# The chunk states of the S5 layers with the inputs held and the table streamed, in two column halves

## The chip, the cores and the metric

The kernel runs on one core of a Trainium2 chip. The metric is device time in microseconds (us) of one execution; the median of three executions of the kernel before is 1205.5 us. TensorE (PE) multiplies, VectorE (DVE) and ScalarE (ACT) do the elementwise work, GpSimd (POOL) a little of it, and the queue of SyncE (SP) starts most transfers.

## What is computed

A network of four layers on 256 tokens of 1024 channels, all in float32. Layers 0 and 3 mix tokens with an S5 state-space mixer, layer 1 with differential attention, layer 2 with pooling; an MLP with a hidden width of 4096 follows each. The S5 mixer, cut to what matters here:

```python
u = h @ w_in                                   # 256 x 1024, 64 groups of 16 channels
bu = einsum('btgh,gph->btgp', u, bbar)         # 64 complex states in each group
x = scan over the tokens of  x[t] = abar * x[t-1] + bu[t]
y = einsum('btgp,ghp->btgh', x.re, c_re) - einsum('btgp,ghp->btgh', x.im, c_im) + d_skip * u
z = gelu(y);  out = (z * sigmoid(z @ w_gate)) @ w_out
```

## The kernel before

The kernel cuts the 256 tokens into 64 chunks of four tokens. For a chunk, a table takes its four inputs to the state that they alone produce; a scan then carries the states over the 64 chunks; a second table takes the carried state, and a third the chunk's own inputs, to the four outputs. Two groups of channels make a pair (2 x 64 states); the 32 pairs are worked in four quarters q of eight pairs.

The order of the work in an S5 layer is written out by hand in the string `SEQ` (line 87); `step` (line 763) emits one word after the other. The words that are spoken of below, each for a quarter q: `g` is half of the product with W_in (`gemm_quarter`, line 239), `V` turns its output into rows of channels (ACT line 794, DVE line 795), `i`, `o`, `s` build tables, `S` turns the state table on TensorE (16 transposes, line 595) and copies it out on ACT (line 598), `T` makes the third table (matmuls at line 618, ACT at 623 and 626, DVE at 624), `m` computes the chunk states (`s5_state`, line 672), `c` carries them (`s5_chain`, line 683), all on DVE, `y` makes the outputs (`s5_out`, line 711: eight times one matmul with T and two with O, one for each half of the 128 output rows, then gelu on ACT at 725 and transposes on DVE at 729), and `z` transposes these on TensorE (copies on ACT at 753). For a half of the columns, `e` is a quarter of the product with W_gate and `w` of that with W_out. In layer 3 the tables are built during earlier MLPs; `K`, `H`, `L` bring them back from memory.

Matmuls go through the helper `mm` (line 142), transposes through `tr` (146), elementwise DVE work through `tt` (151), so most rows of the profile have one of these lines. TensorE executes in the order of `SEQ`; the orders of ACT, DVE and SP are set when the kernel is built, and each engine runs its own list strictly in turn. A matmul of two plain float32 operands appears in the trace as two records, called passes below. The products with large weights are done with operands split in two parts on ACT (line 204) and DVE.

In `s5_state` a slice of the state table is the stationary operand and the chunk inputs V move, 64 columns of them:

```python
self.mm(ps[:, 64 * j:64 * j + 64], self.st[q % 2][:, :, 2 * j + ri], V[:, :, j], start=True, stop=True)
```

The table lies as `st = [128, 128, 16]`, so that a slice `[:, :, 2j + ri]` takes every 16th element of a partition. The result has the states in its 128 rows, as `c` wants it.

Of the kernel before, what the change touches and what calls it, by code (L numbers as in the profile page):

```python
# [16 lines left out]
NT = 2  # L17
# [22 lines left out]
def plan():  # L40
    """Half blocks of 256 rows x 512 columns (array, index, row, column) in the order in which they are used."""
# [34 lines left out]
def whole(name, i, row):  # L76
    """Whether a half block is taken whole instead of split."""
    return name == "s5_w_in" and i == 0 or name == "s5_w_gate" and row < GW[i]


# The order of emission in the S5 layers (0, 1: layers 0 and 3) and in attention (2).
# S5, for the quarter q of the channels: f transposes of the input, p parameters, i/o/s tables and S/T their parts on
# the tensor engine, K/H/L tables brought back, g W_in, V its output in rows of channels, m states, c carries, y outputs,
# z transposes; for the half n of the columns: e gate, w W_out.
# Attention: g and w the products with W_qkv and W_o, l lambda, r transposes, a scores and softmax, t transposes,
# b products with the values, n transposes of the result.
SEQ = {2: "g0 g0 g2 g0 g0 l g2 g2 g2 r00 g1 r20 g1 r01 r21 a01 a00 a10 g1 a11 g3 g3 t00 g1 t01 t10 g3 g3 g4 g4 r10 r30 r31 r11 t11 a02 a13 a03 g4 g4 b00 b01 a12 t03 g5 g5 t13 b11 n00 b10 t02 g5 g5 b03 t12 b13 n10 b02 b12 w0 w1 n01 w1 n11 w0 w0 w0 w1 w1",
       0: "f0 g0 p g2 i0 f1 g1 g0 s0 g1 S0 i1 V0 V1 s1 m0 o1 o0 S1 T0 g2 c0 m1 i2 c1 y0 T1 g3 o2 V2 S2 g3 i3 V3 y1 s2 T2 z0 m2 o3 e0 c2 z1 e1 T3 S3 s3 m3 c3 y2 e1 e0 z2 y3 e0 z3 e1 e0 e1 w0 w0 w0 w1 w0 w1 w1 w1",
       1: "g0 g3 g0 T0 K0 K1 V0 g1 m0 T1 g1 K2 V1 g2 g2 m1 c0 V2 c1 y0 g3 H2 m2 V3 c2 y1 K3 z0 m3 L2 z1 H3 c3 L3 e0 e1 y2 e0 e1 z2 y3 e0 z3 e1 e0 e1 w1 w0 w0 w0 w0 w1 w1 w1"}


class Net:
# [69 lines left out]
    def exp(self, out, x, shape, tag):  # L162
        """exp on the vector engine: 2^n times a polynomial of the rest, its even and its odd terms apart."""
# [26 lines left out]
    def fetch(self):  # L190
        """Loads and splits the half blocks [128, 2, 512] that come next."""
# [23 lines left out]
    def mm3(self, out, sh, sl, mh, ml, start, stop):  # L215
        """out += (sh + sl)^T (mh + ml), of which sl^T ml is below float32's rounding."""
# [6 lines left out]
    def gemm_unit(self, xT, u, banks, first, last):  # L223
        """Both token tiles times a half block of 256 x 512."""
# [14 lines left out]
    def gemm_quarter(self, xT, bank, first, last):  # L239
        """Both token tiles times 512 x 256, side by side in one bank."""  # L240
# [14 lines left out]
    def gemm_T_unit(self, xT, u, banks, first, last):  # L255
        """banks[f // 2][:, f % 2] += (half block of 256 x 512)^T xT for its four column tiles f."""
# [35 lines left out]
    def stat(self, t, n):  # L292
        """The squares of x[t][:, n half] towards the mean square; after both, 1 / rms."""
# [15 lines left out]
    def normed(self, n, t, sub, delay=1.5):  # L309
        """x[t][:, n half] is final for sublayer sub: its operands and statistics."""  # L310
# [11 lines left out]
    def first(self, n):  # L322
        """The same for a half of the input, in whole operands."""
# [80 lines left out]
    def rounded(self, out, a, s):  # L404
        """The integer nearest to a * s."""
# [11 lines left out]
    def s5_put(self, l, q):  # L417
        """Keeps the tables in memory until their layer."""
# [8 lines left out]
    def s5_get(self, l, q, part):  # L427
        """Brings back the tables of one stage: states and inputs (0), carries (1), outputs (2)."""
# [16 lines left out]
    def s5_params(self, l, P):  # L445
        """The discretised parameters, [128 = two groups x 64 states, 32 pairs of groups]."""
# [46 lines left out]
        # powers 4 .. 0 of the discretised eigenvalues, and the factor of the inputs  # L493
# [51 lines left out]
    def products(self, b, wa, wb):  # L545
        """b[0] times wa and b[1] times wb: b [128, 8, 16] over columns and powers, wa and wb [128, 8, 2, 4] over channels."""
# [8 lines left out]
    def s5_in_table(self, l, P, q):  # L555
        """From the inputs of a chunk to its state, for the eight pairs of groups 8 q .. (S)."""
# [21 lines left out]
    def swapped(self, l, q):  # L578
        """Whether the table of the states goes through memory to be turned."""
        return l == 1  # L580

    def s5_late(self, l, q, d=None):
        """The parts of the tables that the tensor engine makes: S from the inputs to the state, T to the outputs."""
# [5 lines left out]
        def states():  # L589
            st = self.st[q % 2]  # L590
            for ri in range(2):
                for b in range(2):
                    ps = self.bank()
                    for j in range(4):
# [36 lines left out]
    def s5_out_table(self, l, P, q):  # L631
        """From the state before a chunk to its outputs."""
# [16 lines left out]
    def s5_small_tables(self, l, P, q):  # L649
        """Phases of the chunks, e^{4 i theta (c - 32)}, and the decay over a chunk, zero where a pair begins."""  # L650
# [21 lines left out]
    def s5_state(self, l, P, q, V):  # L672
        """Eight pairs: the states that the chunks reach, from zero."""
        tb = P[q]
        tb["sb"] = []
        for ri in range(2):
            ps = self.bank()
            for j in range(8):
                self.mm(ps[:, 64 * j:64 * j + 64], self.st[q % 2][:, :, 2 * j + ri], V[:, :, j], start=True, stop=True)
                self.pe(0.213)  # L680
            tb["sb"].append(ps.rearrange("p (j c) -> p j c", j=8))

    def s5_chain(self, l, P, q):
        """Eight pairs: the states carried over the chunks, before each chunk."""
# [26 lines left out]
    def s5_out(self, l, P, q, V):  # L711
        """Eight pairs: outputs, gelu, and the transposes into rows of tokens."""
# [20 lines left out]
    def s5_z(self, l, P, q, zT, zf):  # L733
        """Transposes into rows of channels, as an operand and whole."""
# [20 lines left out]
    def s5(self, l, done):  # L755
# [7 lines left out]
        def step(c, q):  # L763
# [493 lines left out]
```

## Time and profile before

| | |
|---|---|
| times of three executions | 1204.42, 1205.5, 1205.73 us |
| span of the profiled execution | 1204.5 us |
| its TensorE: busy, mean granted clock | 97% of the span, 0.953 |
| its DVE, ACT busy | 67%, 55% |
| chain that ended last: share of TensorE | 94% |
| layer 0's S5 part, layer 3's S5 part | about 22 to 181 us, 866 to 1006 us |

The time of the profiled execution itself is not among the three; its span lies within their range, and the median is 1.0 us above it. The page's first part gives busy time by engine. In the chain of waits each step is followed back to what released it. The timeline lists instructions in order of time with start and length in us, and "x16" merges 16 records. [...]

### The profile page before, as it was taken

How to read it: one execution, taken by the hardware profiler on the slowest of the kernel's cores; microseconds unless marked ns; L12 is line 12 of the kernel's file. 1: busy time of each engine (PE TensorE's matmuls, PEld its weight loads, DVE VectorE, ACT ScalarE, POOL GpSimd, SP SyncE). 2: the span in 40 equal slices, each digit the busy share in tenths (PEclk: the TensorE clock that was granted, in tenths of full speed). 3: DMA queues.
4: the chain of work that ended last, by engine and by line, in shares of the span. 5: the costliest groups of instructions: out<-in, count | busy, mean ns of one | idle time of the engine just before them, and what ended most of it. 6: DMA issues, size and time to landing. Idle time of an engine off the chain costs nothing.

```text
span 1204.5 us, 18922 instructions
## 1 busy us (share of the span) xinstructions
PE 1171.1 (97%) x7192; PEld 1042.7 (87%) x7192; DVE 809.9 (67%) x1488; ACT 663.4 (55%) x1322; POOL 52.3 (4%) x111
## 2 busy tenths in 40 slices
PE   5999999999999999999999999999999999999994
PEld 4989889899888788989888899899898889989983
DVE  7766579857658997986655765655764766655563
ACT  4846367656656676775644754544630156554452
POOL 4002000000000001000000100000100001000000
PEclk9877799999999999999999999999985799999998
DMA  5211256766665444667667365665542256556651
GB/s 150 88 35 36 84 179 188 228 219 208 207 208 168 140 143 154 198 207 217 192 189 232 98 201 180 186 185 185 174 132 79 89 172 195 183 182 189 183 185 58
DMA packets 56635, 196.51 MB, mean 163 GB/s; under 512 B 7136, under 2 KB 7648, under 8 KB 56544
## 3 DMA queue, kind: packets, MB, share of 16 engines
q1 hardware_dynamic: 54528, 189.69, 50.5%
q10 hardware_dynamic: 2016, 5.61, 1.4%
q8 instruction: 56, 0.92, 0.3%
q14 instruction: 35, 0.29, 0.1%
HBM read 188.46 MB, written 6.82 MB: 162 GB/s over the span
## 4 chain that ended last, share of the span: by engine, by line
PE 94%; ACT 2%; DMA 1%; DVE 1%; issue 0%; SPq 0%; POOL 0%; ACTq 0%; POOLq 0%
PE mlp_ps L142 60%; PE mix_ps L142 31%; PE mix_ps L146 2%; DMA start_raw<-in_wts 1%; ACT start_st L598 0%; PE mlp_ps L146 0%; ACT mix_m L885 0%; ACT start_T L626 0%; ACT start_T L623 0%; DVE mix_m L151 0%; SPq L1071 0%; ACT mlp_m L1170 0%; DVE start_x L151 0%; ACT start_ba L575 0%; ACT mix_m L794 0%
## 5 line engine op out<-in xcount | busy, mean ns | idle before, releaser
L151 DVE TENSOR_TENSOR mlp_wlo<-mlp_raw,mlp_whi 128x512 fp32r<-128x512 f32 x492 | 318.5, 686 | 215.9 <-ACT mlp_whi L204 215.7
L204 ACT CAST mlp_whi<-mlp_raw 128x512 fp32r<-128x512 f32 x492 | 281.5, 618 | 255.3 <-PE mlp_ps L142 190.9
L142 PE MATMUL mlp_ps<-mlp_whi,mlp_m 128*128 128x512 f32 x1024 | 327.8, 396 | 0.0
L142 PEld LDWEIGHTS mlp_ps<-mlp_whi,mlp_m 128*128 128x128 f32 x1024 | 192.8, 188 | 45.5
L142 PE MATMUL mlp_ps<-mlp_m,mlp_whi 128*128 128x256 f32 x1248 | 226.2, 283 | 0.0
L142 PE MATMUL mlp_ps<-mlp_wlo,mlp_m 128*128 128x512 f32 x512 | 202.9, 396 | 0.0
L142 PEld LDWEIGHTS mlp_ps<-mlp_m,mlp_whi 128*128 128x128 f32 x1248 | 192.1, 188 | 0.6
L142 PE MATMUL mlp_ps<-mlp_m,mlp_wlo 128*128 128x256 f32 x624 | 175.2, 281 | 0.0
L142 PE MATMUL mlp_ps<-mix_m,mlp_whi 128*128 128x256 f32 x672 | 122.1, 283 | 0.0
L142 PEld LDWEIGHTS mlp_ps<-mlp_m,mlp_wlo 128*128 128x128 f32 x624 | 118.3, 190 | 0.0
L142 PEld LDWEIGHTS mlp_ps<-mlp_wlo,mlp_m 128*128 128x128 f32 x512 | 96.5, 188 | 22.0
L142 PE MATMUL mix_ps<-mix_whi,mix_m 128*128 128x512 f32 (+1 forms) x352 | 108.7, 385 | 0.0
L151 DVE TENSOR_TENSOR mix_wlo<-mix_raw,mix_whi 128x512 fp32r<-128x512 f32 x124 | 81.5, 685 | 38.4 <-ACT mix_whi L204 38.3
L204 ACT CAST mix_whi<-mix_raw 128x512 fp32r<-128x512 f32 x124 | 72.6, 621 | 62.0 <-PE mix_ps L142 35.0
L142 PEld LDWEIGHTS mlp_ps<-mix_m,mlp_whi 128*128 128x128 f32 x672 | 104.5, 188 | 1.8
L142 PE MATMUL mlp_ps<-mix_m,mlp_wlo 128*128 128x256 f32 x336 | 94.5, 281 | 0.0
L142 PEld LDWEIGHTS mix_ps<-mix_whi,mix_m 128*128 128x128 f32 x352 | 66.3, 195 | 13.3 <-issue 0.5
L142 PE MATMUL mix_ps<-mix_wlo,mix_m 128*128 128x512 f32 (+1 forms) x176 | 67.1, 381 | 0.0
L151 DVE TENSOR_TENSOR mlp_m<-mlp_m,mlp_m 128x512 fp32r<-128x512 f32 (+1 forms) x72 | 51.5, 716 | 19.4 <-ACT mlp_m L360 18.6
L142 PEld LDWEIGHTS mlp_ps<-mix_m,mlp_wlo 128*128 128x128 f32 x336 | 63.8, 190 | 0.0
L142 PE MATMUL mix_ps<-mix_m,start_st 128*128 128x64 f32 x256 | 56.9, 398 | 0.4 <-ACT start_st L598 0.3
L142 PEld LDWEIGHTS mix_ps<-mix_m,start_st 128*128 128x128 f32 x256 | 56.4, 311 | 0.9 <-ACT start_st L598 0.9
(324 smaller groups left out, 1523.5 us busy)
## 6 DMA issues: line engine op xcount, KB each, us to landing
mlp_raw<-in_wts SPq DMA_DIRECT2D x252, 512.0 KB, 4.1
mix_raw<-in_wts SPq DMA_DIRECT2D x84, 512.0 KB, 3.6
kept<-mlp_m SPq DMA_DIRECT2D x4, 512.0 KB
start_st<-kept SPq DMA_DIRECT2D x32, 64.0 KB, 3.3
start_x<-in_x SPq DMA_DIRECT2D x4, 256.0 KB
start_raw<-in_wts SPq DMA_DIRECT2D x2, 512.0 KB, 16.8
mlp_m<-in_s5bc SPq DMA_DIRECT2D x2, 512.0 KB, 4.6
kept<-start_O ACTq DMA_DIRECT2D x2, 512.0 KB
```

The source lines that it names most:

```text
L142: i = self.nc.tensor.matmul(*a, **k)
L146: i = self.nc.tensor.transpose(*a)
L151: (eng or self.nc.vector).tensor_tensor(out=out, in0=a, in1=b, op=op)
L204: nc.scalar.copy(hi[:, s], raw[:, s])
```

## The change

The chunk inputs become the stationary operand, 64 columns for a pair, and 256 columns of the table (two parts of 128) move. Two pairs j are put into the lower and the upper 64 columns of the array, and so into rows 0 to 63 and 64 to 127 of one bank; a quarter has eight matmuls of 256 columns instead of sixteen of 64. The result has chunks in its rows; ACT copies it to memory, and a new step `n` (`s5_turn`) turns it with eight transposes. The table is laid out so that 32 neighbours of a moving row lie together, V so that a pair's 64 columns do. In both `SEQ` strings `n` stands some words behind its `m`, and some `c`, `e`, `m` and `y` change places.

```diff
-       0: "... s1 m0 o1 o0 S1 T0 g2 c0 m1 i2 c1 y0 T1 g3 o2 V2 S2 g3 i3 V3 y1 s2 T2 z0 m2 o3 e0 c2 z1 e1 T3 S3 s3 m3 c3 y2 e1 e0 z2 y3 e0 z3 ..."
-       1: "g0 g3 g0 T0 K0 K1 V0 g1 m0 T1 g1 K2 V1 g2 g2 m1 c0 V2 c1 y0 g3 H2 m2 V3 c2 y1 K3 z0 m3 L2 z1 H3 c3 L3 e0 e1 y2 e0 e1 z2 y3 ..."
+       0: "... s1 m0 o1 o0 S1 n0 T0 m1 c0 g2 n1 i2 c1 y0 T1 g3 o2 V2 S2 g3 i3 V3 y1 s2 T2 m2 z0 o3 e0 n2 c2 z1 e1 T3 S3 s3 m3 e1 n3 c3 y2 e0 z2 y3 e0 z3 ..."
+       1: "g0 g3 g0 T0 K0 K1 V0 g1 m0 T1 g1 n0 K2 V1 g2 m1 c0 g2 n1 V2 c1 y0 g3 H2 m2 V3 y1 n2 K3 c2 z0 m3 L2 z1 H3 e0 n3 c3 L3 e1 y2 e0 e1 z2 y3 ..."
...
-                    nc.scalar.copy(st.rearrange("p m (j x) -> p j m x", x=2)[:, 4 * b:4 * b + 4, :, ri],
-                                   ps.rearrange("p (j m) -> p j m", j=4))
+                    nc.scalar.copy(st.rearrange("p a (j x) c -> p j x a c", x=2)[:, 4 * b:4 * b + 4, ri],
+                                   ps.rearrange("p (j a c) -> p j a c", j=4, a=4))
...
     def s5_state(self, l, P, q, V):
+        P[q]["rows"] = S = self.m4([128, 4, 2, 128])
+        for b in range(2):
+            ps = self.bank()
+            for i in range(2):
+                for r in range(2):
+                    j = 4 * b + 2 * i + r
+                    self.mm(ps[64 * r:64 * r + 64, 256 * i:256 * i + 256], V[:, j],
+                            self.st[q % 2][:, :, 2 * j:2 * j + 2].rearrange("p a x c -> p x a c"),
+                            start=True, stop=True, skip_group_check=True)
+                self.pe(0.43)
+            self.nc.scalar.copy(S[:, 2 * b:2 * b + 2].rearrange("p i x m -> p (i x m)"), ps)
+
+    def s5_turn(self, l, P, q):
         tb = P[q]
         tb["sb"] = []
         for ri in range(2):
             ps = self.bank()
-            for j in range(8):
-                self.mm(ps[:, 64 * j:64 * j + 64], self.st[q % 2][:, :, 2 * j + ri], V[:, :, j], start=True, stop=True)
-                self.pe(0.213)
+            for i in range(4):
+                self.tr(ps[:, 128 * i:128 * i + 128], tb["rows"][:, i, ri], self.ident)
+                self.pe(0.113)
...
-                V[q] = self.m2([128, NT, 8, 32])
+                V[q] = self.m2([128, 8, 64])
...
-        self.st = [self.t([128, 128, 16], f"st{b}") for b in range(2)]
+        self.st = [self.t([128, 4, 16, 32], f"st{b}") for b in range(2)]
```

Line numbers of the changed kernel are one to seventeen higher. The built order shows what an engine's list became.

TensorE in layer 0, from the state table of quarter 0 to `y0` (`start_st` is the state table, the first operand is the one that moves; `mix_cad` belongs to `T`). Before:

```order
L142 MATMUL mix_ps_457<-mix_m_125_431,start_st_17_95 128x64 x8
L142 MATMUL mix_ps_466<-mix_m_125_431,start_st_17_95 128x64 x8
L146 MATMUL mix_ps_499<-start_ident_65,start_ba_16_94 128x128 x4
L146 MATMUL mix_ps_505<-start_ident_65,start_ba_16_94 128x128 x4
L146 MATMUL mix_ps_511<-start_ident_65,start_ba_16_94 128x128 x4
L146 MATMUL mix_ps_517<-start_ident_65,start_ba_16_94 128x128 x4
L142 MATMUL mix_ps_525<-mix_cad_487,start_ba_15_93 32x64 x16
```

and after the change:

```order
L143 MATMUL mix_ps_458<-start_st_17_95,mix_m_125_431 64x256 x4
L143 MATMUL mix_ps_464<-start_st_17_95,mix_m_125_431 64x256 x4
L147 MATMUL mix_ps_494<-start_ident_65,start_ba_16_94 128x128 x4
L147 MATMUL mix_ps_500<-start_ident_65,start_ba_16_94 128x128 x4
L147 MATMUL mix_ps_506<-start_ident_65,start_ba_16_94 128x128 x4
L147 MATMUL mix_ps_512<-start_ident_65,start_ba_16_94 128x128 x4
L147 MATMUL mix_ps_518<-start_ident_65,mix_m_134_457 128x128 x4
L147 MATMUL mix_ps_523<-start_ident_65,mix_m_134_457 128x128 x4
L143 MATMUL mix_ps_530<-mix_cad_482,start_ba_15_93 32x64 x16
```

Sixteen matmuls of 64 columns became eight of 256 on half the rows, and the eight transposes of `n0` stand behind those of `S1` and ahead of `T0`.

DVE in layer 0 between `V1` and `c0` (`mix_q_pa`, `mix_q_pb` and `mix_cad` mark the products of the tables `o1` and `o0`; the rows with `mix_ps` begin the carry `c0`; the row on `start_T` is an addition to table T):

```order
L810 STREAM_TRANSPOSE mix_m_127_437<-mix_m_128_438 128x8x32
L158 TENSOR_SCALAR mix_m_130_444<-mix_m_129_443 128x512
L152 TENSOR_TENSOR mix_m_129_443<-mix_m_129_443,mix_m_130_444 128x512
L152 TENSOR_TENSOR mix_m_138_473<-start_m_7_75,mix_q_pa_269 128x1024
L152 TENSOR_TENSOR mix_m_139_474<-start_m_7_75,mix_q_pb_270 128x1024
L152 TENSOR_TENSOR mix_m_141_485<-start_m_7_75,mix_q_pa_269 128x1024
L152 TENSOR_TENSOR mix_cad_470<-mix_m_138_473,mix_m_139_474 128x16x64
L152 TENSOR_TENSOR mix_m_142_486<-start_m_7_75,mix_q_pb_270 128x1024
L152 TENSOR_TENSOR mix_cad_482<-mix_m_141_485,mix_m_142_486 128x16x64
L152 TENSOR_TENSOR mix_m_154_566<-mix_ps_518,mix_ph_383 128x1024
L152 TENSOR_TENSOR start_T_21_99<-start_T_21_99,mix_dd_528 32x16x16
L152 TENSOR_TENSOR mix_m_155_567<-mix_ps_523,mix_ph_383 128x1024
```

All six products now stand between the phases of quarter 1 and `c0`; before the change four of them stood ahead of V's first transposes, and the addition to T behind c0's scans instead of between its first two rows.

ACT in layer 0 behind `T2` and the gelu of `y1` (line 685 copies the rows of `m2`, 768 those of `z0`, which `e0` reads; 576, 627 and 660 to 666 build tables of quarters 2 and 3):

```order
L685 COPY mix_m_203_831<-mix_ps_832 128x512
L576 COPY start_ba_16_94<-mix_m_189_749 64x64x16 x2
L627 COPY start_T_21_99<-start_T_21_99 32x16x48
L627 COPY start_T_21_99<-start_T_21_99 32x16x32
L660 ACTIVATE mix_m_198_794<-mix_m_196_792 128x512
L664 ACT_TABLE_LOAD
L664 ACTIVATE mix_ph_799<-mix_m_196_792 128x512
L665 ACTIVATE mix_ph_799<-mix_m_198_794,start_hpi_88 128x512
L666 ACTIVATE mix_ph_799<-mix_m_196_792 128x512
L627 COPY start_T_21_99<-start_T_21_99 32x16x16
L685 COPY mix_m_203_831<-mix_ps_838 128x512
L768 COPY mix_m_207_849<-mix_ps_844 128x512
```

Before the change the copy of `z0` stood first in this stretch, directly behind T2's second activation.

## Rows read from the trace of the kernel before

**Rows 1.** The page, part 1: busy time, share of the span and instructions of each engine.
```profile
PE 1171.1 (97%) x7192; PEld 1042.7 (87%) x7192; DVE 809.9 (67%) x1488; ACT 663.4 (55%) x1322; POOL 52.3 (4%) x111
```

**Rows 2.** The chain that ended last, in order of time: start, length, engine, count.
```profile
867.92 0.87 PE mix_ps L146 x8
868.80 64.65 PE mix_ps L142 x404
```

**Rows 3.** The state table's tile: duration in ns (min/median/max), first and last start.
```profile
L142 PEld LDWEIGHTS mix_ps<-mix_m,start_st x256: 291/311/338, 38.4 to 940.8; 128*128 128x128 f32 x128
...
L598 ACT COPY start_st<-mix_ps x16: 1005/1070/1130, 37.3 to 116.6; 128x512 f32<-128x512 f32 x16
```

**Rows 4.** Stretches: length, then PE, PEld, DVE, ACT, POOL busy; granted clock; DMA, GB/s.
```profile
866.00:878.50 12.50, 12.50 (x107) 12.41 (x106) 10.14 (x23) 8.87 (x23) 2.97 (x7) 1.00 0.53 169
878.50:885.50 7.00, 7.00 (x34) 6.93 (x32) 2.64 (x4) 1.14 (x2) 0.00 (x0) 0.86 0.27 77
885.50:889.00 3.50, 3.50 (x33) 3.38 (x32) 2.45 (x2) 0.00 (x0) 0.00 (x0) 0.50 0.31 96
905.20:913.40 8.20, 8.20 (x50) 6.36 (x49) 7.01 (x6) 0.00 (x0) 0.13 (x1) 0.50 0.21 64
950.30:955.30 5.00, 5.00 (x50) 3.90 (x48) 3.98 (x6) 0.00 (x0) 0.00 (x0) 0.99 0.37 111
```

**Rows 5.** Timeline of TensorE: a `g` in whole operands (16 passes); `T3` (32 passes).
```profile
51.70 3.72 PE L142 MATMUL mix_ps<-mix_raw,mix_m 128*128 128x256 f32 x16
110.93 1.97 PE L142 MATMUL mix_ps<-mix_cad,start_ba 128*32 128x64 f32 x32
```

**Rows 6.** Timeline of TensorE, 950.62 to 950.65 us: the passes that had begun.
```profile
950.63 0.28 PE L142 MATMUL mix_ps<-mix_m,start_O 128*64 128x64 f32 x2
```

**Rows 7.** Timeline of TensorE inside `y2`, at the full clock.
```profile
951.52 0.43 PE L142 MATMUL mix_ps<-mix_m,start_T 128*128 128x64 f32 x2
951.89 0.34 PE L142 MATMUL mix_ps<-mix_m,start_O 128*64 128x64 f32 x4
952.15 0.32 PE L142 MATMUL mix_ps<-mix_m,start_T 128*128 128x64 f32 x1
```

**Rows 8.** Timeline of ACT in layer 0: copies, activations, a table load.
```profile
41.05 3.76 ACT L645 COPY start_O<-mix_cad 64x512 f32<-64x512 f32 x6
51.81 1.25 ACT L623 ACTIVATE start_T<-mix_ps,start_gmask 32x512 f32<-32x512 f32 x2 [1.10 <-PE mix_ps L142]
53.59 1.87 ACT L626 COPY start_T<-start_T 32x768 f32<-32x768 f32 x3
96.08 2.10 ACT L575 COPY start_ba<-mix_m 64x1024 f32<-64x1024 f32 x2
100.74 1.28 ACT L663 ACT_TABLE_LOAD   x1
107.58 0.59 ACT L753 COPY mix_m<-mix_ps 128x512 f32<-128x512 f32 x1 [1.39 <-PE mix_ps L146]
```

**Rows 9.** Timeline of DVE: V1's transposes; first and last instructions of the carry `c3`.
```profile
37.12 0.81 DVE L795 STREAM_TRANSPOSE mix_m<-mix_m 128x256 f32<-128x256 f32 x2 [0.45 <-ACT mix_m L794]
943.36 2.35 DVE L151 TENSOR_TENSOR mix_m<-mix_ps,mix_ph 128x1024 f32<-128x1024 f32 x2
...
951.60 2.75 DVE L151 TENSOR_TENSOR mix_m<-mix_m,mix_m 64x504 f32<-64x504 f32 x4
```

**Rows 10.** Timeline of TensorE: the starts of `y0`, `e0`, `y3` in layer 0, `y0`, `y3` in layer 3.
```profile
62.07 0.64 PE L142 MATMUL mix_ps<-mix_m,start_T 128*128 128x64 f32 x2
101.61 5.49 PE L142 MATMUL mix_ps<-mix_m,mix_raw 128*128 128x256 f32 x16
140.60 0.33 PE L142 MATMUL mix_ps<-mix_m,start_T 128*128 128x64 f32 x2
905.23 0.64 PE L142 MATMUL mix_ps<-mix_m,start_T 128*128 128x64 f32 x2
964.39 0.33 PE L142 MATMUL mix_ps<-mix_m,start_T 128*128 128x64 f32 x2
```

More of the change, by code (lines that the diff above doesn't have):

```diff
@@ L87 @@
 SEQ = {2: "g0 g0 g2 g0 g0 l g2 g2 g2 r00 g1 r20 g1 r01 r21 a01 a00 a10 g1 a11 g3 g3 t00 g1 t01 t10 g3 g3 g4 g4 r10 r30 r31 r11 t11 a02 a13 a03 g4 g4 b00 b01 a12 t03 g5 g5 t13 b11 n00 b10 t02 g5 g5 b03 t12 b13 n10 b02 b12 w0 w1 n01 w1 n11 w0 w0 w0 w1 w1",
-       0: "f0 g0 p g2 i0 f1 g1 g0 s0 g1 S0 i1 V0 V1 s1 m0 o1 o0 S1 T0 g2 c0 m1 i2 c1 y0 T1 g3 o2 V2 S2 g3 i3 V3 y1 s2 T2 z0 m2 o3 e0 c2 z1 e1 T3 S3 s3 m3 c3 y2 e1 e0 z2 y3 e0 z3 e1 e0 e1 w0 w0 w0 w1 w0 w1 w1 w1",
-       1: "g0 g3 g0 T0 K0 K1 V0 g1 m0 T1 g1 K2 V1 g2 g2 m1 c0 V2 c1 y0 g3 H2 m2 V3 c2 y1 K3 z0 m3 L2 z1 H3 c3 L3 e0 e1 y2 e0 e1 z2 y3 e0 z3 e1 e0 e1 w1 w0 w0 w0 w0 w1 w1 w1"}
+       0: "f0 g0 p g2 i0 f1 g1 g0 s0 g1 S0 i1 V0 V1 s1 m0 o1 o0 S1 n0 T0 m1 c0 g2 n1 i2 c1 y0 T1 g3 o2 V2 S2 g3 i3 V3 y1 s2 T2 m2 z0 o3 e0 n2 c2 z1 e1 T3 S3 s3 m3 e1 n3 c3 y2 e0 z2 y3 e0 z3 e1 e0 e1 w0 w0 w0 w1 w0 w1 w1 w1",
+       1: "g0 g3 g0 T0 K0 K1 V0 g1 m0 T1 g1 n0 K2 V1 g2 m1 c0 g2 n1 V2 c1 y0 g3 H2 m2 V3 y1 n2 K3 c2 z0 m3 L2 z1 H3 e0 n3 c3 L3 e1 y2 e0 e1 z2 y3 e0 z3 e1 e0 e1 w1 w0 w0 w0 w0 w1 w1 w1"}
 class Net:
@@ L566, in s5_in_table @@
             self.halves(lambda g, p: nc.scalar.copy(ba[p].rearrange("p j x k g h -> p (j x) k g h")[:, :, 3, g], d[p, :, 3]))
-            m = self.m4([128, 2, 32, 16])
-            nc.vector.transpose(out=m.rearrange("p i c f -> p f i c"),
+            m = self.m4([128, 2, 16, 32])
+            nc.vector.transpose(out=m.rearrange("p i f c -> p f i c"),
                                 in_=d.rearrange("p f (i k) h -> p f i (k h)", i=2))
             self.count += 1
-            P["swap", q] = self.dram.tile([128, 2, 32, 16], F32, name=f"kept_{self.count}")
+            P["swap", q] = self.dram.tile([128, 2, 16, 32], F32, name=f"kept_{self.count}")
             nc.sync.dma_start(out=P["swap", q], in_=m)
@@ L597, in states @@
                         self.pe(0.113)
-                    nc.scalar.copy(st.rearrange("p m (j x) -> p j m x", x=2)[:, 4 * b:4 * b + 4, :, ri],
-                                   ps.rearrange("p (j m) -> p j m", j=4))
+                    nc.scalar.copy(st.rearrange("p a (j x) c -> p j x a c", x=2)[:, 4 * b:4 * b + 4, ri],
+                                   ps.rearrange("p (j a c) -> p j a c", j=4, a=4))
         def fetch():
             st = self.st[q % 2]
-            kept = self.tables[l]["swap", q].rearrange("(b k h) i c f -> b k h i (c f)", b=4, k=2)
+            kept = self.tables[l]["swap", q].rearrange("(b k h) i f c -> b k h i (f c)", b=4, k=2)
             for k in range(4):
@@ L606, in fetch @@
                     r = 32 * k + 16 * g
-                    nc.sync.dma_start(out=st[r:r + 16, 64 * g:64 * g + 64].rearrange("p (b c) f -> p b (c f)", b=2),
+                    nc.sync.dma_start(out=st[r:r + 16, 2 * g:2 * g + 2].rearrange("p b f c -> p b (f c)"),
                                       in_=kept[2 * g:2 * g + 2, k % 2, :, k // 2].rearrange("b h f -> h b f"))
@@ L717, in s5_out @@
             o = ps[:, 64 * j:64 * j + 64]
-            self.mm(o, tb["T"][:, j].rearrange("p g x -> p (g x)"), V[:, :, j], start=True, stop=False,
+            self.mm(o, tb["T"][:, j].rearrange("p g x -> p (g x)"), V[:, j], start=True, stop=False,
                     skip_group_check=True)
@@ L794, in step @@
                     nc.scalar.activation(out=u[:, s], in_=win[q][:, s], func=AF.Copy, scale=self.rstd[t])
-                    nc.vector.transpose(out=V[q][:, t].rearrange("p j c -> p (j c)"), in_=u[:, s])
+                    nc.vector.transpose(out=V[q][:, :, 32 * t:32 * t + 32], in_=u[:, s].rearrange("p (j c) -> p j c", j=8))
             elif c == "m":
                 self.s5_state(l, P, q, V[q])
+            elif c == "n":
+                self.s5_turn(l, P, q)
             elif c == "c":
```

## The prediction

> **What bounds the kernel now.** I read the page first, then the chain of waits, then the state table's own rows, then the S5 stretches one by one. The page shows TensorE busy 97% of the span and DVE 67% [rows 1]; a mean over the span says little about two S5 parts of some 140 us each, so the chain decides. It runs through TensorE for 94% of the span, and layer 3's S5 part is one unbroken piece of it, 404 passes in 64.65 us from 868.8 us [rows 2]: there a microsecond less of TensorE is a microsecond less of the kernel, until something else comes late. In layer 0 the chain also passes through ACT's table copies.
>
> The rows of the state table [rows 3] show what the change is aimed at. The 128 matmuls of `m` are 256 weight loads, two for each matmul, of 0.311 us each. One stretch `m0` of layer 3 (32 passes) fills 878.5 to 885.5 us at a mean granted clock of 0.86 [rows 4]; with its last passes it is 7.05 us, 0.22 us a pass for 64 columns that move. A pass of 256 columns costs as much: 16 in 3.72 us [rows 5]. So a state pass is paced by its weight load, which picks every 16th element. All eight `m` together are 8 x 7.05 = 56.4 us.
>
> [...]
>
> **The change, part by part.** *`m` itself.* A quarter now has 8 matmuls of 256 columns, 16 passes. In series at 0.22 us they are 3.6 us; in pairs 1.8 us. The trace of before shows such pairs: the O matmuls of `y` also write the two halves of the rows, and in a window of 0.03 us two of their passes have begun, with one duration of 0.28 us [rows 6]. I take the pairs as concurrent. Entering and leaving the half-width form costs something: in `y2` a period of two T passes and four O passes is 0.63 us (951.52 to 952.15) [rows 7], where two full weight loads at 0.11 (the spacing of the transposes, 8 in 0.87 us [rows 2]) and two O pairs at 0.055 (half the columns) come to 0.33; the rest, 0.30, is two switches. So `m` = 1.8 + 0.3 = 2.1 us at the full clock, some 3.8 at half. [...]
>
> *`n`.* Eight transposes, 0.87 us [rows 2], 1.74 at half clock. TensorE's saving at the full clock is 7.05 - 2.1 - 0.87 = 4.1 us a quarter, 33 us for all eight: 1172 us if all of it lay on the path.
>
> *ACT.* Two copies of 0.59 (128x512 out of PSUM, as for `z` [rows 8]) are added for each quarter. The four copies of the turned table in layer 0 took 1.07 each while they wrote single elements 64 bytes apart [rows 3]; they now write runs of 32, so I take 0.55, the spacing of plain copies; the other bound is no gain, 0.92 apart. V's transposes and copies, the transfers of the table (2 KB runs as before) and the words of the weight plan, whose order stays, I cost at nothing: they move the same bytes, behind TensorE's `g`.
>
> *The walk through layer 3.* The question is what is late once `m` is short. `m0` starts at 878.5 as before and ends at 880.6; `T1` at the full clock is 1.9 [rows 5]; the split `g` is 24 passes at 12.5/107 = 0.117 [rows 4], 2.8; `n0` ends at 886.2. But V1 stands on ACT behind T1's activations and copies (1.25 + 0.35 on DVE + 1.87 [rows 8]): 882.5 + 3.5 = 886.0, then V1, 0.8 on DVE [rows 9], and a weight split stand ahead of `c0`, an estimate of 1.9 by the 0.59 of a plain copy and two such on DVE: 888.7. The carry is nine DVE operations, 943.36 to 954.35, 11.0 us [rows 9]: `y0` can start at 899.8, 5.4 us before today's 905.23 [rows 10]. TensorE has by then been idle since about 894.6, so I give `y0` 8.2 us (the 0.50 row): 908.0. A `g` while the clock comes back (4.5) and `m2` (2.1) lead to 914.6; `c1` is done at 899.8 + 11.0 + 1.1 for transposes between = 911.9 and hidden. `y1` 5.5 us (the clock falling inside) to 920.1. Then `n2`, `z0`, `m3`, `z1` at mostly half clock 1.7 + 0.9 + 3.8 + 0.6 to 927.1, `e0` 4.0, `n3` 0.9, `e1` 3.7 (16 passes each [rows 5]) to 935.7; `c2` starts with `n2` at 921.9 and, 11.8 us long, ends at 933.7, hidden. `y2` 5.2, `e0` and `e1` 7.4 with 1.7 for the clock behind `y2`, `z2` 0.5: `y3` starts at 950.5, against 964.39 [rows 10]. Behind it the words are the same. Gain **13.9 us**.
>
> *The walk through layer 0.* Here TensorE is not alone, and the built order of DVE and ACT hurts. V1's transposes end at 37.9 [rows 9]; with the phases between them DVE is free at 39.4 and now has all six products of `o1` and `o0` ahead of `c0`, 1.13 each (a carry's first two rows are 2.35 for two): 46.2. ACT does the table copies (2.2, from 37.4), four phase operations (2.2 from 39.5), `m0`'s two copies (1.1), the next table (2.2), then eight O copies at 0.62 (six took 3.76 [rows 8]) = 5.0 to 50.0, and T's two activations 1.25: 51.3. DVE's second row of `c0` stands behind the addition to T, which waits for just that: 51.6, then 9.8 us of the carry, and `y0` starts at 61.4, against 62.07. The 16 us that TensorE would have saved by then end in idleness, and the clock is 0.50 again: `y0` 8.2, `T1` 3.5 to 73.1, then `g`, `S2`, `g` 4.1 + 1.8 + 3.6 to 82.6 for `y1`; it ends near 88.2, `T2` at 91.7. Now `e0` waits for the copy of `z0`, which stands behind: T's activations and a gelu 1.85, `m2`'s copies 1.1, the table copies 2.1, T's copies 1.87, phases 2.3, a table load 1.28, its own 0.59 [rows 8], together 11.1: 102.8, against 101.61 [rows 10]. From there `e0` 5.5, `n2` 0.9, `z1` 0.4, `e1` 3.6, `T3` 1.9, `S3` 1.8, its copies 1.1, `m3` 2.1, `e1` 3.6, `n3` 0.9: 124.6; `c3` (11.0 + 1.2 of weight splits) lets `y3` start at 136.8, against 140.60. Gain **3.8 us**.
>
> Sum: 1204.5 - 13.9 - 3.8 = 1186.8 us for the profiled execution's span, which the median exceeds by 1.0; rounding for waits that I rated at their worst, I forecast **1187 us**.
>
> **The rivals.** *The clock holds.* If TensorE's pauses before the two `y0` do not end in the 0.50 state, `y0` and `y1` of layer 3 gain 3.2 and the steps behind `y1` about 3; in layer 0 `T2` ends some 8 us earlier and `e0` with it: 1187 - 6 - 8 = 1173. For it: the stretch before `m0` ran at 1.00 throughout, and `m` itself, in which the clock fell, is now a third as long. Against it: `y` by itself brought the clock down [rows 4].
>
> *The halves do not overlap.* Then `m` is 3.6 + 0.3 and each one on the path (`m0`, `m2`, `m3` of layer 3, `m3` of layer 0) costs 1.8 more, 7 us: 1194. Against it stand the O passes [rows 6]. [...]
>
> *The table moves slowly.* Place: `m`. The moving rows come in four runs of 32 elements, with 512 elements from run to run; if that paces a pass as the picked weights did (0.22 for 64 columns, 0.88 for 256, in pairs 0.44), `m` stays at 7.1, and `n` adds 8 x 0.87 = 7 and `c0`'s later start (899.8 + 5) takes the rest: 1204.5 + 7 + 3 = 1214. It is slower from `m` above 7.05 - 0.87 = 6.2 us on. Runs of 32 moved in V before without showing in `y`.
>
> *ACT and DVE swallow it.* If the table copies stay at 0.92, `y0` of layer 0 moves to 64.4 and all behind it by 3; with a like delay on ACT in layer 3 the result is 1200 to 1206. That the change is not made is excluded: TensorE's built list has the 64x256 rows.
>
> **How the numbers follow.** Forecast 0.52, clock holds 0.22, no overlap 0.15, slow table 0.06, swallowed 0.05. A measurement of this kernel tells 0.2%, 2.4 us, from no change. Faster: the first three and a third of the last, 0.91; same 0.03; slower 0.06. The forecast's own range is 1181 to 1193 (copies, half-clock stretches). Reaching to most of the clock case and to no overlap, 1173 to 1196 holds about 0.8.
>
> **What would show it.** Right: `m` of 1.9 to 2.3 us (near 4 at 0.50) with two 64-column passes beginning together; the table copies near 0.6; DVE waiting for ACT inside `c0` of layer 0; TensorE idle 4 to 7 us ahead of both `y0` and ahead of `e0` in layer 0, at 0.50 behind; `y3` near 137 and 950. Wrong: `m` above 3.5; no idle time ahead of `y0`; or the MLP stretches changed, on which nothing here bears.

## The result, and the profile after

The changed kernel takes **1185.65 us** in the median of four executions (1182.96 to 1187.43), the kernel before 1204.96: a ratio of 0.9839, 95% interval 0.9821 to 0.9857. The profiled execution took 1185.03 us with a span of 1183.2, against 1204.5 before; 21.3 us are to be explained. (Line numbers of the changed kernel are up to 17 higher: 142, 146 and 598 are now 143, 147 and 599.)

The page's busy line, to be read beside [rows 1]:

```profile
PE 1127.8 (95%) x7128; PEld 993.6 (84%) x7128; DVE 807.2 (68%) x1488; ACT 665.1 (56%) x1338; POOL 47.2 (4%) x111
```

The rows of the state table's tile (duration in ns, min/median/max, then first and last start), beside [rows 3]:

```profile
L143 PEld LDWEIGHTS mix_ps<-start_st,mix_m x128: 132/137/137, 40.5 to 921.9; 128*64 128x64 f32 x128
L143 PE MATMUL mix_ps<-start_st,mix_m x128: 379/379/431, 40.5 to 922.2; 128*64 128x256 f32 x128
...
L599 ACT COPY start_st<-mix_ps x16: 557/598/628, 38.9 to 118.0; 128x512 f32<-128x512 f32 x16
```

TensorE's busy time fell by 43.3 us, but the span by half of that. A load, now of 64 columns, is under half of what it was (0.137 us against 0.311), and a copy 0.56 of it. The timeline of TensorE, first in layer 3 around `m0`, then the waits in both layers and the two `y3` (start, length, and in brackets the idle time ahead and who ended it):

```profile
876.74 1.95 PE L143 MATMUL mix_ps<-start_st,mix_m 128*64 128x256 f32 x16
878.61 1.97 PE L143 MATMUL mix_ps<-mlp_cad,start_ba 128*32 128x64 f32 x32
...
48.12 1.95 PE L143 MATMUL mix_ps<-mix_cad,start_ba 128*32 128x64 f32 x32 [2.88 <-DVE mix_cad L152]
61.52 0.44 PE L143 MATMUL mix_ps<-mix_m,start_O 128*64 128x64 f32 x2 [4.88 <-DVE mix_m L152]
102.23 6.52 PE L143 MATMUL mix_ps<-mix_m,mix_raw 128*128 128x256 f32 x16 [8.54 <-ACT mix_m L768]
137.22 0.33 PE L143 MATMUL mix_ps<-mix_m,start_T 128*128 128x64 f32 x2
...
896.79 0.44 PE L143 MATMUL mix_ps<-mix_m,start_O 128*64 128x64 f32 x2 [3.52 <-DVE mix_m L152]
943.12 0.33 PE L143 MATMUL mix_ps<-mix_m,start_T 128*128 128x64 f32 x2
```

`m0` is 1.95 us instead of 7.05, and `T1` behind it runs at a granted clock of 1.00 in 1.97 us, where it had 0.50 and took 3.5. In return TensorE waits for `o0`'s products, for `c0` (twice) and 8.5 us for the copy of `z0`, all in places where it did not wait before.

The stretches from the start of an S5 part to its `y3` show the balance (length, then PE, PEld, DVE, ACT, POOL busy; granted clock; DMA, GB/s): layer 0 and layer 3, first of before, then of after.

```profile
21.60:140.60 119.00, 117.23 (x661) 103.96 (x661) 83.28 (x100) 69.07 (x111) 15.23 (x19) 0.78 0.16 51
878.50:964.40 85.90, 85.90 (x479) 78.13 (x478) 52.05 (x64) 14.18 (x26) 0.38 (x3) 0.72 0.29 97
```

```profile
21.40:137.20 115.80, 96.81 (x628) 79.89 (x629) 85.11 (x103) 68.77 (x122) 11.03 (x19) 0.84 0.21 62
876.70:943.10 66.40, 62.01 (x445) 52.08 (x445) 51.09 (x63) 18.66 (x34) 0.37 (x3) 0.87 0.39 120
```

In layer 0 TensorE is busy for 20.4 us less, and idle for 19.0 us where it was for 1.8: the part is 3.2 us shorter (3.4 between the two `y3`). In layer 3 the part is 19.5 us shorter, although TensorE now idles for 4.4 us in it, and the clock is 0.87 instead of 0.72.

The first `g` of layer 0, which stands ahead of everything that the change touches, differs too (before, then after):

```profile
21.61 3.72 PE L142 MATMUL mix_ps<-start_raw,mix_m 128*128 128x256 f32 x16 [3.62 <-DMA start_raw<-in_wts]
21.44 5.41 PE L143 MATMUL mix_ps<-start_raw,mix_m 128*128 128x256 f32 x16 [3.61 <-DMA start_raw<-in_wts]
```

From 22.6 to 26.0 us its granted clock was 1.00 before and 0.50 after. This is no effect of the change: in the run g3_first below, which has the changed kernel's words in layer 0, it was 1.00, and in whole_slices, which has the old ones, 0.50. So layer 0's part would be some 1.7 us shorter still if the two executions had begun alike.

Behind `y3` of layer 0 some 1.6 us are lost again, most of which the windows explain (before, then after):

```profile
145.60:149.00 3.40, 3.40 (x30) 3.40 (x30) 1.46 (x3) 1.96 (x4) 0.00 (x0) 1.00 0.17 57
```

```profile
142.10:145.40 3.30, 3.30 (x19) 3.21 (x16) 0.77 (x2) 0.60 (x1) 0.00 (x0) 0.50 0.02 5
```

The first of the split products behind `y3` run at a granted clock of 0.50 after the change and at 1.00 before: 24 passes take 4.4 us instead of 3.0. 3.4 - 1.6 + 19.5 = 21.3 us.

### The profile page after: what moved, and what is told of

It is laid out like the page before. It is cut to its first block, busy times and chain, and to the rows that moved or that the text cites. A ratio compares the mean times of both kernels' runs of the same rounds, so it can differ in the third digit from the quotient of the medians.

```text
span 1183.2 us, 18807 instructions
## 1 busy us (share of the span) xinstructions
PE 1127.8 (95%) x7128; PEld 993.6 (84%) x7128; DVE 807.2 (68%) x1488; ACT 665.1 (56%) x1338; POOL 47.2 (4%) x111
## 4 chain that ended last, share of the span: by engine, by line
PE 89%; DVE 4%; ACT 3%; DMA 1%; issue 1%; SPq 0%; POOL 0%; DVEq 0%; ACTq 0%; POOLq 0%
PE mlp_ps L143 62%; PE mix_ps L143 25%; DVE mix_m L152 2%; PE mix_ps L147 2%; DMA start_raw<-in_wts 1%; DVE mix_m L712 1%; ACT start_T L627 0%; ACT start_T L624 0%; PE mlp_ps L147 0%; ACT start_O L646 0%; ACT mix_m L902 0%; DVE mix_wlo L152 0%; ACT start_st L599 0%; SPq L1088 0%; ACT mlp_m L1187 0%
## 5 line engine op out<-in xcount | busy, mean ns | idle before, releaser
L152 DVE TENSOR_TENSOR mix_m<-mix_m,mix_m 64x504 f32<-64x504 f32 (+3 forms) x72 | 55.2, 776 | 3.1 <-ACT mix_m L833 2.3
L361 ACT CAST mlp_m<-mlp_m 128x512 fp32r<-128x512 f32 x64 | 39.6, 620 | 22.9 <-DVE mlp_m L152 22.8
```

The costliest lines, as they stand in the source:

```text
L152: (eng or self.nc.vector).tensor_tensor(out=out, in0=a, in1=b, op=op)
L361: nc.scalar.copy(oh, s)
```

## The experiments

All twelve runs, each timed in three rounds beside the kernel before on the same chip; the ratio to it is given with its interval.

| run | us | ratio |
|---|---|---|
| whole_slices | 1165.79 | 0.9663 (0.9633 to 0.9693) |
| halves_in_turn | 1186.39 | 0.9840 (0.9824 to 0.9855) |
| strided_moving | 1200.81 | 0.9954 (0.9940 to 0.9968) |
| old_order | 1186.12 | 0.9834 (0.9820 to 0.9849) |
| ws_new_order | 1162.69 | 0.9645 (0.9621 to 0.9669) |
| z0_early | 1188.02 | 0.9841 (0.9804 to 0.9878) |
| g3_first | 1186.94 | 0.9854 (0.9824 to 0.9884) |
| both_words | 1186.23 | 0.9855 (0.9822 to 0.9889) |
| no_turn | 1159.12 | 0.9601 (0.9576 to 0.9625) |
| turn_unread | 1183.36 | 0.9818 (0.9791 to 0.9845) |
| c0_first | 1185.67 | 0.9824 (0.9805 to 0.9844) |
| stride8 | 1162.70 | 0.9644 (0.9620 to 0.9668) |

**1. Only the layout: whole_slices.** The kernel before, its table as `[128, 16, 128]` (the transfers of layer 3 are split to match).

```diff
-        self.st = [self.t([128, 128, 16], f"st{b}") for b in range(2)]
+        self.st = [self.t([128, 16, 128], f"st{b}") for b in range(2)]
...
-                self.mm(ps[:, 64 * j:64 * j + 64], self.st[q % 2][:, :, 2 * j + ri], V[:, :, j], start=True, stop=True)
+                self.mm(ps[:, 64 * j:64 * j + 64], self.st[q % 2][:, 2 * j + ri], V[:, :, j], start=True, stop=True)
```

> The kernel before, with one thing changed: the state table lies as [128, 16, 128], so that each stationary slice of m is one unbroken run of 128 (no stride); the matmuls stay 64 columns wide and the order of the work is the old one. Theory of the prediction (a state pass was paced by its weight load, and the load by its stride): m falls from 7.05 to 32 x 0.11 = 3.5 to 3.8 us, the table copies of layer 0 from 1.07 to 0.6; layer 3 gains some 4 x 3.4 = 13.6 and layer 0 about 2, so 1190 us, 1187 to 1194. Rival (a float32 pass costs 0.22 us whatever moves and however the weights lie, so that only fewer passes or pairs of them help): m stays at 7.05, 1203 to 1206.

Measured 1165.8 us: 40 below before, and 20 below the changed kernel. The execution that was profiled, 1160.88 us, is the fastest of the four. The table's tile:

```profile
L142 PEld LDWEIGHTS mix_ps<-mix_m,start_st x256: 186/192/338, 41.0 to 897.6; 128*128 128x128 f32 x128
```

the timeline at `m0` and `T1` of layer 3:

```profile
858.06 3.68 PE L142 MATMUL mix_ps<-mix_m,start_st 128*128 128x64 f32 x32
861.67 1.97 PE L142 MATMUL mix_ps<-mlp_cad,start_ba 128*32 128x64 f32 x32
```

and the stretches of layers 0 and 3:

```profile
21.80:118.60 96.80, 95.43 (x661) 83.69 (x661) 82.70 (x100) 62.20 (x110) 15.42 (x19) 0.88 0.20 62
858.10:917.50 59.40, 59.40 (x479) 54.31 (x478) 51.35 (x64) 14.21 (x26) 0.38 (x3) 0.97 0.47 134
```

The load takes 0.192 us instead of 0.311 and `m` 3.68 instead of 7.05: the stride was the cost. Eight such `m` are 27 us; in layer 3 the rest comes with the clock: its part has the same instructions as before, no idle time in either kernel, and is 26.5 us shorter, 13.5 of it in `m`, while its mean clock went from 0.72 to 0.97. My 1190 had the 13.5 and left out the clock; in layer 0 it allowed 2 us, and the part came out 22.2 us shorter (96.8 instead of 119.0). TensorE is idle 1.4 us in layer 0 and not at all in layer 3, against 19.0 and 4.4 in the changed kernel.

**2. How strong a stride: stride8.** whole_slices with the table as `[128, 8, 128, 2]`.

```diff
-                self.mm(ps[:, 64 * j:64 * j + 64], self.st[q % 2][:, 2 * j + ri], V[:, :, j], start=True, stop=True)
+                self.mm(ps[:, 64 * j:64 * j + 64], self.st[q % 2][:, j, :, ri], V[:, :, j], start=True, stop=True)
```

> The kernel whole_slices with the table as [128, 8, 128, 2]: a stationary slice now takes every second element (8 bytes apart) instead of an unbroken run, where the kernel before took every 16th (64 bytes). Theory A (any stride breaks the load, or one of 8 bytes costs half of what one of 64 costs): m between 5 and 7 us, 1180 to 1206. Theory B (a load with a stride of 8 bytes is as quick as an unbroken one): m 3.7 us, 1161 to 1168.

The table's tile:

```profile
L142 PEld LDWEIGHTS mix_ps<-mix_m,start_st x256: 193/196/337, 39.0 to 898.2; 128*128 128x128 f32 x128
```

1162.7 us and 0.196 us a load, as theory B has it. 8 bytes from element to element cost next to nothing here (0.196 us a load against 0.192), 64 bytes nearly double the time of `m` (7.05 against 3.68); strides between the two were not tried.

**3. The same stride in the moving operand: strided_moving.** The changed kernel with the old table layout.

```diff
-        self.st = [self.t([128, 4, 16, 32], f"st{b}") for b in range(2)]
+        self.st = [self.t([128, 128, 16], f"st{b}") for b in range(2)]
...
-                            self.st[q % 2][:, :, 2 * j:2 * j + 2].rearrange("p a x c -> p x a c"),
+                            self.st[q % 2][:, :, 2 * j:2 * j + 2].rearrange("p m x -> p x m"),
```

> The changed kernel with the state table in its old layout [128, 128, 16], so that every moving element is 64 bytes from the next and the table copies of layer 0 write single elements again. Theory (the stride hurts weight loads alone): m stays 1.95 and only the copies of layer 0 go back from 0.55 to 1.07 apart, 2 us on ACT per quarter, of which 2 to 3 us come on the path: 1186 to 1189. Rival (a moving read with a stride is as slow as a picked weight, the prediction's rival of the slow table): m about 7, 8 x 5 us on TensorE of which some 20 to 28 on the path: 1206 to 1214.

`m0` of layer 3 in the timeline, and the table's tile:

```profile
889.78 3.76 PE L143 MATMUL mix_ps<-start_st,mix_m 128*64 128x256 f32 x16
```

```profile
L599 ACT COPY start_st<-mix_ps x16: 1027/1072/1109, 39.0 to 126.3; 128x512 f32<-128x512 f32 x16
```

1200.8 us, between my two cases: `m` is 3.76 us, about twice 1.95, so this moving read suffers from 64 bytes as the load does, though it does not reach 7. 15 us of the change's 19 hang on its new layout, the table copies of layer 0 included.

**4. The pairs: halves_in_turn.** The loops over `i` and `r` of `s5_state` exchanged.

```diff
-            for i in range(2):
-                for r in range(2):
+            for r in range(2):
+                for i in range(2):
```

> The changed kernel, but in each bank the two matmuls of the lower half are issued before the two of the upper half, so that neighbours in program order write the same half. Theory (passes start in program order, so only the passes at the change of halves begin together): m 2.8 to 3.8 instead of 1.95, on the path in m0, m2, m3 of layer 3 and m3 of layer 0, so 4 to 7 us more than the changed kernel: 1190 to 1193. Rival A (each half has its own line of matmuls, and the later one need not wait its turn): m stays near 1.95, 1185.6. Rival B (no overlap was at work at all and the passes are merely quick): m stays 1.95 too, but then no two passes begin within 0.01 us of each other.

Measured 1186.4 us, as rival A has it. `m0` of layer 3, and a window from 876.69 to 876.72 us:

```profile
876.70 2.00 PE L143 MATMUL mix_ps<-start_st,mix_m 128*64 128x256 f32 x16
...
876.70 0.44 PE L143 MATMUL mix_ps<-start_st,mix_m 128*64 128x256 f32 x2
```

`m0` is 2.00 us, and two passes have begun within 0.03 us although each half's matmuls now stand two in a row in the program. The records do not name the half of a pass, so one more rival has to be met: a pair could be the two passes of one matmul. Then the exchange would leave the distance within a pair alone. But the first pair of `m0` begins 7 ns apart in the changed kernel (876.735 and 876.742), where the other half's first pass is the third in the program, and 13 ns apart here (876.699 and 876.712), where it is the fifth. So the pairs are most likely one pass of each half, they need not be neighbours, and the matmuls of the two halves do not keep strictly to the order of TensorE's list.

**5. The order of the words: old_order, ws_new_order.** The changed kernel with the words of before and each `n` behind its `m`; and whole_slices with the words of the change.

```diff
-       1: "g0 g3 g0 T0 K0 K1 V0 g1 m0 T1 g1 n0 K2 V1 g2 m1 c0 g2 n1 V2 c1 y0 ..."
+       1: "g0 g3 g0 T0 K0 K1 V0 g1 m0 n0 T1 g1 K2 V1 g2 g2 m1 n1 c0 V2 c1 y0 ..."
```

> The changed kernel with the words of both SEQ strings in the order of before, each n put directly behind its m. Theory (the order matters little beside the matmuls: TensorE waits some 0.8 to 1.3 us at each n for ACT's copy, and layer 3's y1 has c2 ahead of it on DVE again, while in layer 0 z0's copy is early again): 1187 to 1193. Rival A (the new order is free of effect): 1185 to 1187. Rival B (the order brings half of the gain or more): 1195 or above. Rival C (the new order costs time in layer 0, where e0 now waits 8.5 us for ACT): below 1184.

> The kernel whole_slices (the kernel before with unbroken table slices, 1165.8 us) with the words of both SEQ strings in the order of the change, the n left out. Theory (the 20 us between it and the changed kernel are the price of the extra stage: the copies on ACT and the transposes between m and c, with the waits and the half clock that follow; the order of the words adds little): 1163 to 1170. Rival (the new order of the words is what holds the changed kernel back, whichever way m is done): 1178 to 1186.

1186.1 and 1162.7 us: either way of doing `m` takes about the same time under either order. The words neither made the gain nor hold the changed kernel back. The granted clock does differ: layer 3's part of ws_new_order, from `m0` to `y3`,

```profile
860.50:924.60 64.10, 64.10 (x478) 57.76 (x477) 51.68 (x64) 14.09 (x25) 0.38 (x3) 0.89 0.45 126
```

has no idle time and loads without a stride, like that of whole_slices, but ran at 0.89 and not at 0.97, and took 64.1 us instead of 59.4.

**6. The waits one by one: z0_early, g3_first, both_words, c0_first.** Words of the changed kernel exchanged, in layer 0 (first) and in layer 3.

```diff
- ... T2 m2 z0 o3 e0 ...
+ ... T2 z0 m2 o3 e0 ...
...
- ... c1 y0 g3 H2 m2 ...
+ ... c1 g3 y0 H2 m2 ...
...
- ... m0 T1 g1 n0 K2 V1 g2 m1 c0 g2 n1 ...
+ ... m0 T1 n0 c0 g1 K2 V1 g2 m1 g2 n1 ...
```

> The changed kernel with two words of layer 0 exchanged, z0 m2 for m2 z0, so that ACT's list has the copy of z0 directly behind the activations of T2 again. Theory (e0 of layer 0 waits 8.5 us for that copy): e0 starts near 94 instead of 102.2, but n2 behind it still waits for the copies of m2's rows, which stay behind the tables on ACT, until some 102.7 instead of 108.6; all that follows comes 5 to 6 us earlier: 1179 to 1182. Rival (c3 or the tables of quarter 3 are late as well, so that the wait only moves to T3, m3 or y2): 1184 to 1187.

> The changed kernel with two words of layer 3 exchanged, g3 y0 for y0 g3, so that the 3.1 us of g3 fill TensorE's wait for c0 ahead of y0. Theory (TensorE waits 3.5 us there, and the granted clock falls to 0.50 in that wait): 3 us from the wait alone, up to 8 if the clock then stays at 1.00 through y0 and g3: 1178 to 1183. Rival (the time is lost elsewhere, since c1, y1 and z0 wait for DVE in turn): 1184 to 1187.

> The changed kernel with both exchanges, z0 m2 in layer 0 and g3 y0 in layer 3. Theory: the sum of the two, 8 to 14 us under the changed kernel: 1172 to 1178; it stays above the 1165.8 of whole_slices, since the copies, the transposes and the wait for c0 in layer 0 (4.9 us) remain. Rival (the waits move on): 1181 or above.

> The changed kernel with n0 c0 put directly behind T1 in layer 3, so that DVE's list has c0 ahead of V1's transposes, as the kernel before and whole_slices have it. Theory (the late c0 is what makes TensorE wait 3.5 us before y0, and the clock falls in that wait): c0 begins near 882 instead of 886.84, y0 runs without a wait, 4 us from that and up to 5 more if the clock stays at 1.00: 1176 to 1182. Rival (the wait moves on to y1 or the clock falls all the same): 1184 to 1187.

None gained: 1188.0, 1186.9, 1186.2, 1185.7. (One execution of z0_early took 1180.1 us; the other three took 1187.4 to 1189.0.) Each did what it was to do in its place, and a wait came up in the next. TensorE's waits of z0_early:

```profile
102.62 2.88 PE L147 MATMUL mix_ps<-start_ident,mix_m 128*128 128x128 f32 x12 [4.40 <-ACT mix_m L685]
132.69 0.69 PE L147 MATMUL mix_ps<-start_ident,mix_m 128*128 128x128 f32 x2 [2.59 <-DVE mix_m L744]
```

of g3_first:

```profile
909.64 0.44 PE L143 MATMUL mix_ps<-mix_m,start_O 128*64 128x64 f32 x2 [3.27 <-DVE mix_m L152]
```

and of c0_first:

```profile
890.04 3.68 PE L143 MATMUL mix_ps<-start_st,mix_m 128*64 128x256 f32 x16 [3.30 <-issue]
```

In z0_early `e0` starts at 94.5 instead of 102.2, but `n2` then waits 4.4 us for the copies of `m2`'s rows and `z2` 2.6 us for DVE. In g3_first `y0` waits 1.7 us instead of 4.4, and `y1`, which did not wait, now waits 3.3 us for `c1`. In c0_first the carry starts at 880.7 instead of 886.8 and `y0` does not wait; V1's transposes now stand among c0's rows on DVE (884.7 and 889.5), and `m1`, which needs them, waits 3.3 us. That it waits for them is my reading: the row names no releaser ("issue"), but the second transpose ends at 889.9 and `m1` begins at 890.04.

**7. The extra stage: no_turn, turn_unread.** Without copies and transposes, the carry fed from m's banks; and with both in place, but the carry fed from m's banks all the same.

```diff
-            self.nc.scalar.copy(S[:, 2 * b:2 * b + 2].rearrange("p i x m -> p (i x m)"), ps)
+            tb["sb"].append(ps.rearrange("p (j c) -> p j c", j=8))
```

> The changed kernel without its extra stage: neither the copies of the rows nor the transposes n are there, and the carry reads the banks of m as they come (the turning of the states is left out, so what it computes is not the states). The words keep the new order; the lists of DVE and ACT are built anew. Theory (the faster m is worth more than whole_slices has, 1.95 against 3.68 us a quarter, and the extra stage gives it back): some 8 x 1.7 = 14 us below whole_slices, so 1148 to 1158. Rival (DVE's carries or the order of the words hold the kernel back, not the stage): 1165 to 1180.

> The changed kernel with copies and transposes kept in place, but the carry reads the banks of m (as in no_turn, the states are not turned for it); the lists of DVE stay as in the changed kernel but for one row. So all the work of the stage is there and only its being waited for is gone. Theory (in the changed kernel c0 of layer 3 begins at 886.84 because DVE's list has V1 and a weight split ahead of it, and not because n0 is late; e0 of layer 0 waits for ACT's list): 1180 to 1187, near the changed kernel. Rival (the round trip from TensorE over ACT and back is itself what the carries wait for): 1160 to 1174.

1159.1 and 1183.4 us. The stretches of no_turn in layers 0 and 3:

```profile
21.00:116.30 95.30, 87.11 (x597) 71.41 (x597) 83.50 (x101) 65.49 (x116) 15.65 (x19) 0.91 0.24 73
858.60:916.50 57.90, 56.24 (x413) 45.75 (x413) 50.97 (x63) 14.33 (x26) 0.38 (x3) 0.91 0.43 137
```

Leaving the stage out is worth 26.5 us (1185.65 to 1159.12; by the ratios, nearer 29); only ceasing to wait for it 2.3, within the intervals of the two runs. In turn_unread TensorE waits as long ahead of `y0` of layer 3 as in the changed kernel (3.52 us),

```profile
895.21 0.45 PE L143 MATMUL mix_ps<-mix_m,start_O 128*64 128x64 f32 x2 [3.52 <-DVE mix_m L152]
```

and in layer 0 4.88 us ahead of `y0` and 8.53 ahead of `e0`, again as there. So the round trip through ACT is not what the carries wait for. What costs is having the stage at all: its 8 x 0.87 us of TensorE, its sixteen copies on ACT and the lists of DVE and ACT as they are built around it, which differ between the two kernels. The runs do not part these three. no_turn came out just above my 1148 to 1158: of the 14 us by which its eight `m` are shorter than those of whole_slices, 6.7 come through, and TensorE is idle for some 8 us in layer 0.

## Why the prediction was right, and where two errors met

**`m`, `n` and the copies** hold. 1.95 us for `m` against 2.1; from `m0` to `T1` it is 1.87; a pass of 256 columns takes 0.215 (16 of `e0` from 922.96 to 926.41), eight pairs 1.72, so 0.15 us beyond the pairs lie behind the first pass; another 0.1 lies ahead of it, since `m0` begins 0.21 us behind the last pass of `g`, where passes of `g` are 0.117 apart. Together some 0.25, where I had estimated 0.3 from the `y2` period. That this is what two switches of form cost was my reading of what that period leaves over; the runs show the time and not what it goes into. The eight transposes of `n` are 1.04 with their tail, the table copies 0.51 apart (four in 2.05).

**The walk through layer 0** holds in each milestone: `y0` 61.52 (61.4), `e0` 102.23 (102.8), `y3` 137.22 (136.8), with the waits that I had read from the built order: DVE with six products ahead of `c0` and then waiting for T's activations, and ACT with the copy of `z0` behind the tables. The rows of DVE's wait, of `c0`'s second row and of its end, then those of ACT:

```profile
52.50 0.41 DVE L152 TENSOR_TENSOR start_T<-start_T,mix_dd 32x256 f32<-32x256 f32 x1 [3.40 <-ACT start_T L624]
52.84 1.21 DVE L152 TENSOR_TENSOR mix_m<-mix_ps,mix_ph 128x1024 f32<-128x1024 f32 x1
60.00 2.77 DVE L152 TENSOR_TENSOR mix_m<-mix_m,mix_m 64x504 f32<-64x504 f32 x4
```

```profile
101.11 0.58 ACT L685 COPY mix_m<-mix_ps 128x512 f32<-128x512 f32 x1
101.59 0.59 ACT L768 COPY mix_m<-mix_ps 128x512 f32<-128x512 f32 x1
```

The first milestone was met by luck. The slow first `g` of this execution put everything back, so that `c0`'s second row began at 52.84 (51.6) and the carry ended at 62.77 (61.4). But `y0`'s first O passes need only the first two of the carry's last four rows, which I had not counted on: they begin 1.25 us before the carry ends, and `y0` then stops for 0.87 us more. What failed is the step behind `y3`, that the words after it take what they took: the granted clock was 0.50 there from 142.1 to 145.4 us, and 1.6 us were lost.

**The walk through layer 3** holds up to `y1`. Shifted by the 1.76 us by which `m0` starts earlier, `y0`'s first O pass is at 898.6 (899.8) and `y1` at 914.3 (914.6). The carry starts where I had put it, behind V1 and a weight split on DVE:

```profile
885.63 1.29 DVE L152 TENSOR_TENSOR mix_wlo<-mix_raw,mix_whi 128x512 fp32r<-128x512 f32 x2
886.84 2.35 DVE L152 TENSOR_TENSOR mix_m<-mix_ps,mlp_ph 128x1024 f32<-128x1024 f32 x2
```

Behind `y1` the term "mostly half clock" failed. The windows of `y0`, of `n2` to `e1`, and of the two `e` behind `y2`:

```profile
896.80:905.80 9.00, 8.13 (x47) 6.18 (x47) 8.89 (x10) 1.91 (x2) 0.00 (x0) 0.50 0.37 96
918.00:930.70 12.70, 12.70 (x75) 10.82 (x73) 11.29 (x13) 3.45 (x6) 0.12 (x1) 0.91 0.38 126
935.70:942.70 7.00, 7.00 (x35) 6.12 (x34) 6.95 (x11) 1.62 (x3) 0.00 (x0) 1.00 0.22 77
```

`y0` ran at 0.50 as forecast, but from `n2` to `e1` TensorE had 0.91, and 1.00 in the last two `e`: 12.7 us where I had 15.6, and 7.0 where I had 9.1. `y3` came 5.6 us earlier than my walk. So half of the rival in which the clock holds came true: its condition did not, since both `y0` ran at 0.50, but the steps behind `y1`, which it priced at about 3 us, gave 5. 13.9 became 19.5 and 3.8 became 1.8 (3.4 less 1.6). That the sum, 21.3 against 17.7, came out so near is partly luck: 5.6 us too little in layer 3 and 2.0 too much in layer 0 cancel in part. That a pause ends at 0.50 was an assumption of mine, which no row of before shows: both `y0` bear it out, behind waits of 4.88 and 3.52 us, but `T0` of layer 0 ran at 1.00 (1.95 us) behind one of 2.88. No run isolates what brings the clock down.

**The rivals.** No overlap is excluded by run 4, and with it a start strictly in program order, the theory of that run: by it only three pairs could have formed there, and `m0` would be near 13 x 0.215 = 2.8 us; it is 2.00. Nor does that order fit my own reading of [rows 6]: if its two passes belong to the two halves, then the second half's first pass began before the second pass of the first half's matmul, which stands ahead of it in the program. That `y` by itself brought the clock down, which I held against the first rival, is not in [rows 4]: `y0` had 0.50 from its start there and `y2` 0.99. In the kernel before the clock did fall within `y1` of layer 0, which had 0.82 from 84.4 to 90.3 us with 0.50 behind it, but `y3` of layer 0 had 1.00 from 140.6 to 145.6 and 1.00 behind it. The slow table is shown by run 3, at half of the price I gave it: the change avoids it by its layout. That ACT and DVE swallow it rested on table copies 0.92 apart, and is out with their 0.51, though ACT and DVE are late all the same: what they cost here are the idle times above.

**What I did not see** is that the term I called "a state pass is paced by its weight load, which picks every 16th element" was the whole case. I costed the new form against a load that could itself be had at 0.11 us (32 passes in 3.68 us in whole_slices), and so never priced the smaller edit, which gains twice as much.

## What to carry to other kernels

When a load or a moving read takes much longer than its like (here 0.311 us a load against 0.192, 3.76 us an `m` against 1.95), look at its stride first: a layout with 4 or 8 bytes from element to element instead of 64 gave 40 us and more here, without another instruction on TensorE. Turning the product's result cost more here than its transposes, 8 x 0.87 = 7 us of TensorE: the extra stage gave back 26 us or more. Moving a word moved the wait in z0_early, g3_first and c0_first; compare busy time, idle time and granted clock by stretch before believing in a single one.

## What the hardware showed that was not expected

A float32 weight load of 128x128 took 0.311 us from elements 64 bytes apart, 0.192 unbroken and 0.196 at 8 bytes; the moving reads of 256 columns took twice as long at 64 bytes (`m` 3.76 against 1.95). Matmuls on the two halves of the columns began together (7 to 13 ns apart) even with another matmul between them in the program, as far as the records, which do not name the half, allow to say. And the granted clock of layer 3's part differed from kernel to kernel: 0.72 before, 0.87 after the change, 0.97 in whole_slices. That TensorE neither waited nor read with wide strides in whole_slices does not explain it alone, for neither did it in ws_new_order, at 0.89; and the first `g` of layer 0 was at 1.00 in some executions (that of before among them) and at 0.50 in others (that of the changed kernel). What decides it stays open.
